# The S5 mixer of a two-layer trunk: u of tiles 4 to 7 prepared earlier, gelus of tiles 2 and 3 one by one, and another order of GEMM steps and u

## The chip, the cores and the metric

The kernel runs on one core of a Trainium2 chip. The metric is the device time of one execution in microseconds (us), as the median of several runs. TensorE (PE) multiplies, ScalarE (ACT) and VectorE (DVE) work element by element, GpSimd (POOL) does a little, and SyncE (SP) issues most of the DMAs. Each engine works through its own instructions in the order in which they were written, and waits at an instruction until the semaphores that it names are high enough.

## The reference

A trunk of two layers on a sequence of 256 positions and a width of 2048, each layer a token mixer and an MLP. Layer 0 has differential attention, layer 1 an S5 mixer (a grouped diagonal state space):

```python
h = rmsnorm(x, norm_mix[1])
u = h.reshape(B, S, 128, 16)                                  # 128 groups of 16 channels
bu_re, bu_im = einsum('sgc,gpc->sgp', u, bb_re), einsum('sgc,gpc->sgp', u, bb_im)
x_re, x_im = associative_scan(...)                            # x[s] = a * x[s-1] + bu[s], complex, 64 states a group
y = einsum('sgp,gcp->sgc', x_re, cr) - einsum('sgp,gcp->sgc', x_im, ci) + d_skip * h
val, gate = split(gelu(y) @ w_glu, 2)                         # 2048 x 4096
x = x + val * sigmoid(gate)
x = x + relu(rmsnorm(x) @ w1)**2 @ w2
```

## The kernel before

All GEMMs stream their weights from DRAM through one list of chunks (two k-tiles of 128 rows by 512 columns, 512 KB). A chunk lands in `raw`, ScalarE casts it to `wh`, VectorE subtracts to get the remainder `wl`, and TensorE multiplies in three passes (L201 to L203, or L265 and L269 in the MLP's first half). A chunk is prepared up to three ahead of its use. While a GEMM runs, `pump()` is called at each k-tile and steps generators in the list `side`: these lay other work (attention heads, norms, the S5 tables) between the GEMM's instructions. What stands where is thus set by the order in which the Python code runs, with the delays that the generators yield.

The S5 mixer works on 16 tiles of 128 channels. The 256 positions of a tile are 64 chunks of 4. For tile j:

- `s5_u(j)` makes u for tiles j and j+1: four transposes of the residual (L1029), or, when it is given `diag`, four f32 matmuls with a diagonal of the norm's factors (L1031), into one PSUM bank; then 16 ScalarE copies (L1036) that spread it to the tile `vsb`. In the MLP the norm's factors aren't known yet, and `s5_scale` multiplies them in later on VectorE (L107).
- `s5_e(j)` is 16 matmuls (L1056) into one PSUM bank, and then 12 VectorE instructions: multiplications by a table, two scans (L1066), and the state `bc`, which is X[j].
- `s5_y` is 24 matmuls a tile (L1089) from u and X into a bank of its own ring, and at the end of its group 16 gelus (L1096) and a cast (L1100) on ScalarE. `s5_rest` makes the remainder on VectorE.
- `s5_dk(j)` is one ScalarE copy (L1020) that the scan of tile j reads. `s5_fetch(j)` loads the tables of tile j.
- The norm ahead of the mixer (`norm2`) takes two squares with sums on ScalarE (L422) behind each output block of the MLP.
- `glu_tile(j)` is the GEMM step of tile j: 4 f32 matmuls of 128x512 (L1122) with the gelus of tile j as the stationary operand, for the first 512 columns of value and gate.

`s5_phase` puts these in order, in a loop over j. A step has e of tile j+1, the remainder of tile j-3, a GEMM step (none at j = 0, 1 and 4), y of tile j, the copy for tile j+4, the gelus if tile j ends its group, u if j is 2, 4, 6 or 8, and the fetch of tile j+4. The three GEMM steps that are left over follow the loop. In the first two steps `keep_warm` adds 8 matmuls whose result nobody reads, and 18 and 4 stand at the phase's start.

In this phase `bank()` and `s5_u` take PSUM banks 4 and 5 in turn (`rings["sd"]`), so of e and u each takes the bank that the one before the last had. Tiles 0 to 3 get their u in the first MLP's last quarter (`early_u`, spawned by `done0` when the first of the four output blocks is finished); tiles 4 to 7 get it at the phase's start with banks of the ring "acc"; tiles 8 to 15 in the loop.

Of the kernel before, what the change touches and what calls it, by code (L numbers as in the profile page):

```python
# [16 lines left out]
P = 128  # L17
# [19 lines left out]
NCH = S // L  # L37
# [5 lines left out]
LAG = 3  # L43
# [14 lines left out]
def tile_trunk(  # L58
# [7 lines left out]
    v = nc.vector  # L66
# [13 lines left out]
    def nm(s):  # L80
        uid[0] += 1
        return f"{s}_{uid[0]}"
# [5 lines left out]
    def ring(kind):  # L88
        r = rings[kind]
        turn[kind] = (turn[kind] + 1) % len(r)  # L90
        return psum.tile([P, 512], F32, tag=f"bank{r[turn[kind]]}", name=nm(kind), bufs=1)
# [6 lines left out]
    def bank():  # L98
        return ring("sd")

    def tmp(shape, tag, bufs=None, dt=F32):
        if bufs is None:
            return sb.tile(shape, dt, tag=tag, name=nm(tag))
        return sb.tile(shape, dt, tag=tag, name=nm(tag), bufs=bufs)

    def mult(o, a, b):
        v.tensor_tensor(out=o, in0=a, in1=b, op=ALU.mult)  # L107

    def add(o, a, b):
        v.tensor_tensor(out=o, in0=a, in1=b, op=ALU.add)  # L110

    def sub(o, a, b):
        v.tensor_tensor(out=o, in0=a, in1=b, op=ALU.subtract)  # L113

    def tsc(o, a, s1, op0, s2=None, op1=None):
        if op1 is None:
            v.tensor_scalar(out=o, in0=a, scalar1=s1, scalar2=None, op0=op0)
        else:
            v.tensor_scalar(out=o, in0=a, scalar1=s1, scalar2=s2, op0=op0, op1=op1)
# [8 lines left out]
    def spawn(gen, delay=0):  # L128
        side.append([clock[0] + delay, gen])
# [11 lines left out]
    def until(cond):  # L141
        while not cond():
            assert side
            pump()
# [79 lines left out]
    def new_accs():  # L224
        return [ring("acc") for _ in range(NT)]
# [94 lines left out]
    def keep_warm(n):  # L320

        if n == 0:
            return
        a = ring("acc")
        for _ in range(n):
            pe.matmul(a, x1[3].h[:, 0, 0:P], x1[3].h[:, 0:2], start=True, stop=True)
# [683 lines left out]
    def s5_rooms():  # L1010

        for _ in range(4):
            dks.append(tmp([P, Q, NCH], "s1k", bufs=4))
            xps.append(tmp([P, 2, Q, NCH], "bc", bufs=4))
            pool_e.memset(dks[-1][:, :, 0:1], 0.0)
            pool_e.memset(xps[-1][:, :, :, 0:1], 0.0)

    def s5_dk(j):
        if j < NJ:
            act.copy(dks[j % 4][:, :, 1:], rr[:, j * Q:(j + 1) * Q, None].broadcast_to([P, Q, NCH - 1]))  # L1020

    def s5_u(j, diag=None, kind="sd"):

        ps = ring(kind).rearrange("p (i s) -> p i s", s=S)
        for i in range(2):
            for t in range(NT):
                o, xs = ps[:, i, t * P:(t + 1) * P], xres[t][:, (j + i) * P:(j + i + 1) * P]
                if diag is None:
                    pe.transpose(o, xs, ident)  # L1029
                else:  # L1030
                    pe.matmul(o, xs, diag[:, t], start=True, stop=True)  # L1031
        u = tmp([P, 2, Q, NCH], "vsb", bufs=4)
        pv = ps.rearrange("p i (k s) -> p i s k", s=L)
        for s in range(L):
            for q in range(Q):
                act.copy(u[32 * s:32 * s + 32, :, q], pv[32 * q:32 * q + 32, :, L - 1 - s])  # L1036
            yield s
        if diag is None:
            U[j] = u
        else:  # L1040
            U[j], U[j + 1] = u[:, 0], u[:, 1]

    def s5_scale(j, factor):
        u = U[j]
        uv = u.rearrange("p i q k -> p (i q) k")
        mult(uv, uv, factor[:, None, :].broadcast_to([P, 2 * Q, NCH]))
        U[j], U[j + 1] = u[:, 0], u[:, 1]

    def s5_e(j):
        te, to, tt, ct = tab[j]  # L1050
        u, dk, xp = U[j], dks[j % 4], xps[j % 4]
        pe_ = bank().rearrange("p (i q k) -> p i q k", i=2, q=Q)
        for i in range(2):
            for q in range(Q):
                for h in (slice(0, GP), slice(GP, P)):
                    pe.matmul(pe_[h, i, q], te[:, i, q, h], u[:, q], start=True, stop=True)  # L1056
        sh = [P, 2, Q, NCH]
        tw = tmp([P, 2] + sh[1:], "c5")
        t1, t2 = tw[:, 0], tw[:, 1]
        mult(t1, pe_, ct[:, 0:1].broadcast_to(sh))  # L1060
        mult(t2, pe_, ct[:, 1:2].broadcast_to(sh))
        add(t1[:, 0], t1[:, 0], t2[:, 1])
        sub(t1[:, 1], t1[:, 1], t2[:, 0])
        zz = tmp(sh, "s2k", bufs=7)
        for i in range(2):
            v.tensor_tensor_scan(out=zz[:, i].rearrange("p q k -> p (q k)"), data0=dk.rearrange("p q k -> p (q k)"),  # L1066
                                 data1=t1[:, i].rearrange("p q k -> p (q k)"), initial=0.0,
                                 op0=ALU.mult, op1=ALU.add)
        n = NCH - 1
        shn = [P, 2, Q, n]  # L1070
        w1, w2 = tmp(sh, "s2k", bufs=7), tmp(sh, "s2k", bufs=7)
        mult(w1[:, :, :, 0:n], zz[:, :, :, 0:n], ct[:, 0:1, :, 0:n].broadcast_to(shn))
        mult(w2[:, :, :, 0:n], zz[:, :, :, 0:n], ct[:, 1:2, :, 0:n].broadcast_to(shn))
        sub(xp[:, 0, :, 1:], w1[:, 0, :, 0:n], w2[:, 1, :, 0:n])
        add(xp[:, 1, :, 1:], w1[:, 1, :, 0:n], w2[:, 0, :, 0:n])
        X[j] = xp
# [30 lines left out]
    def s5_rest(j):  # L1107

        while rest and rest[0][0] <= j:
            _, blk, kk, n, g = rest.pop(0)  # L1110
            sub(blk.l[:, kk:kk + n], g[:, 0:n], blk.h[:, kk:kk + n].bitcast(F32))
            blk.ready = kk + n == KB
# [16 lines left out]
    def s5_phase(norm):  # L1129
        until(lambda: norm.done)  # L1130
        act.activation(warm_act, warm_act, AF.Gelu_apprx_tanh)
        keep_warm(WARM[0])
        sel = wp.tile([P, 2, NT, P], F32, tag="wl", name="sel", bufs=LIVE)
        ar, diag = sel[:, 0], sel[:, 1]
        for t in reversed(range(NT)):
            tsc(ar[:, t], sela.rearrange("p s r -> p (s r)"), norm.rstd[:, t:t + 1], ALU.mult)
        for t in range(NT):
            act.activation(diag[:, t], ident, AF.Copy, scale=norm.rstd[:, t:t + 1])
        prs = bank()[:, 0:NCH]
        for t in range(NT):  # L1140
            pe.matmul(prs, ar[:, t], selb[:, t], start=(t == 0), stop=(t == NT - 1))
        keep_warm(WARM[1])
        s5_scale(0, prs)
        s5_scale(2, prs)
        s5_e(0)
        for j in (4, 6):
            for _ in s5_u(j, diag, "acc"):
                pass
        groups = [(0,), (1,), (2, 3), (4, 5), (6, 7), (8, 9), (10, 11), (12, 13), (14,), (15,)]
        ys = {}  # L1150
        for grp in groups:
            gen = s5_y(grp)
            for j in grp:
                ys[j] = (gen, j == grp[-1])
        glu = 0
        for j in range(NJ):
            if j + 1 < NJ:
                s5_e(j + 1)
            s5_rest(j - 3)
            if j < 2:  # L1160
                keep_warm(WARM[2])
            if j in (2, 3) or j >= 2 + LAG:
                if glu == 0:
                    A["v"], A["g"] = new_accs(), new_accs()
                glu_tile(glu)
                glu += 1
            gen, end = ys[j]
            next(gen)
            s5_dk(j + 4)
            if end:  # L1170
                for _ in gen:
                    pass
            if j in (2, 4, 6, 8):
                for _ in s5_u(j + 6, diag):
                    pass
            s5_fetch(j + 4)
            pump()
        while glu < NJ:
            prep(GLU0 + 16 + glu - NJ + LAG)
            glu_tile(glu)  # L1180
            glu += 1
        s5_rest(NJ)
# [92 lines left out]

    def done0(u, ts):
        norm2.block(u, ts)
        if u == 0:
            spawn(early_u(), 4)
            spawn(early_tables(), 2)  # L1280
        if u == NB - 1:
            norm2.finish(slice(ts[0], ts[0] + 1))

    def early_u():
        for j in (0, 2):
            for _ in s5_u(j):
                yield 2
        s5_rooms()
        yield 2
        for j in range(4):  # L1290
            s5_dk(j)
            yield 2
# [28 lines left out]
    def evict_gate(accs, vs, u):  # L1321
# [6 lines left out]
        spawn(xT_block(x3[u], u, 2, norm3, "a"), 6)  # L1328

    s5_phase(norm2)  # L1330
    evict_gate(A["g"], first_vals, 0)
    for u in range(1, NB):
# [62 lines left out]
```

## Time and profile before

| | us |
|---|---|
| median of 3 runs | 2104.28 (2104.16 to 2104.45) |
| the profiled execution | 2101.04 |
| its span, from the first instruction to the last | 2099.3 |
| TensorE busy in the span | 2076.1 (99%) |
| VectorE busy | 1369.1 (65%) |
| ScalarE busy | 1061.4 (51%) |
| GpSimd busy | 122.9 (6%) |

The profiled execution lies 3.2 us below the median. A busy share is an average over the whole span: the S5 phase, some 120 us of it, has another mix than the GEMMs around it. The profile's granted clock of TensorE is 0.999 in the mean.

### The profile page before, as it was taken

The page shows a single profiled execution, that of the slowest core. Times are in us where ns is not written, and L with a number is a line of the kernel's source. Part 1 is how long each engine was busy: PE and PEld are TensorE (multiplying, and loading weights), DVE is VectorE, ACT ScalarE, POOL GpSimd, SP SyncE. Part 2 cuts the span into 40 slices and gives each one's busy share as a digit, 9 for nine tenths or more (in the row PEclk, how much of TensorE's full clock was granted, in tenths as well). Part 3 has the DMA queues.
Part 4 walks back from the last instruction along what each step waited for, and adds up shares of the span by engine and source line. Part 5 has one row for each costly group of instructions (what it writes and reads, how often), then busy time and mean ns, then how long its engine had stood idle before and what let it go on. Part 6 is the DMA issues. An engine that isn't in the chain of part 4 may idle for free.

```text
span 2099.3 us, 31788 instructions
## 1 busy us (share of the span) xinstructions
PE 2076.1 (99%) x12126; PEld 1763.8 (84%) x12126; DVE 1369.1 (65%) x2292; ACT 1061.4 (51%) x1640; POOL 122.9 (6%) x210
## 2 busy tenths in 40 slices
PE   8999999999999999999999999999999999999998
PEld 8899998888888888888887668888888888888886
DVE  5785656688678767767866865565556645645655
ACT  5545545555445444454566875444434434434443
POOL 2000200021021002100110000000000000000000
PEclk9999999999999999999999999999999999999999
DMA  7457765677776777687678765665565556555653
GB/s 244 157 193 241 248 178 184 214 229 267 237 240 233 273 238 222 225 276 235 208 266 310 274 215 187 200 201 199 189 195 189 189 193 191 178 204 181 200 192 131
DMA packets 230813, 452.57 MB, mean 216 GB/s; under 512 B 20818, under 2 KB 29348, under 8 KB 230660
## 3 DMA queue, kind: packets, MB, share of 16 engines
q1 hardware_dynamic: 217824, 415.29, 59.8%
q0 software_dynamic: 11440, 32.86, 4.9%
q10 hardware_dynamic: 1396, 2.39, 0.3%
q8 instruction: 95, 1.56, 0.3%
q14 instruction: 58, 0.48, 0.1%
HBM read 420.85 MB, written 41.68 MB: 220 GB/s over the span
## 4 chain that ended last, share of the span: by engine, by line
PE 91%; ACT 3%; DVE 3%; DMA 1%; issue 1%; SPq 0%; DVEq 0%; ACTq 0%
PE acc L265 21%; PE acc L201 15%; PE acc L202 15%; PE acc L203 15%; PE acc L269 11%; PE acc L1122 3%; PE acc L248 2%; PE acc L250 2%; PE acc L249 2%; DVE wl L113 1%; ACT wh L191 1%; PE y L1089 1%; ACT s2k L1096 1%; DMA raw<-in_a_w_in_dram 1%; ACT vsb L1036 1%
## 5 line engine op out<-in xcount | busy, mean ns | idle before, releaser
L113 DVE TENSOR_TENSOR wl<-raw,wh 128x1024 fp32r<-128x1024 f32 (+1 forms) x690 | 833.2, 1217 | 574.4 <-ACT wh L191 570.0
L191 ACT CAST wh<-raw 128x1024 fp32r<-128x1024 f32 (+1 forms) x690 | 712.9, 1047 | 631.0 <-PE acc L203 341.4
L201 PE MATMUL acc<-wh,x 128*128 128x512 f32 x832 | 326.8, 393 | 0.0
L203 PE MATMUL acc<-wh,x 128*128 128x512 f32 x832 | 324.0, 389 | 0.0
L202 PE MATMUL acc<-wl,x 128*128 128x512 f32 x832 | 324.0, 389 | 0.0
L265 PE MATMUL acc<-x,wh 128*128 128x512 f32 x1024 | 273.9, 394 | 2.8 <-DVE s2k L110 2.8
L265 PE MATMUL acc<-a,wh 128*128 128x512 f32 x1024 | 272.8, 393 | 0.0
L201 PE MATMUL acc<-wh,a 128*128 128x512 f32 x640 | 251.5, 393 | 0.0
L202 PE MATMUL acc<-wl,a 128*128 128x512 f32 x640 | 249.4, 390 | 0.1
L203 PE MATMUL acc<-wh,a 128*128 128x512 f32 x640 | 249.3, 390 | 0.0
L265 PEld LDWEIGHTS acc<-x,wh 128*128 128x128 f32 x1024 | 177.3, 189 | 28.9 <-DVE s2k L110 3.2
L265 PEld LDWEIGHTS acc<-a,wh 128*128 128x128 f32 x1024 | 177.3, 189 | 25.3 <-ACT s2k L1324 0.4
L203 PEld LDWEIGHTS acc<-wh,x 128*128 128x128 f32 x832 | 156.2, 188 | 32.9
L201 PEld LDWEIGHTS acc<-wh,x 128*128 128x128 f32 x832 | 156.3, 188 | 32.0 <-ACT vsb L1317 0.3
L202 PEld LDWEIGHTS acc<-wl,x 128*128 128x128 f32 x832 | 156.3, 188 | 31.8 <-issue 0.2
L269 PEld LDWEIGHTS acc<-a,wl 128*128 128x128 f32 x1024 | 152.8, 190 | 18.7
L269 PEld LDWEIGHTS acc<-x,wl 128*128 128x128 f32 x1024 | 152.4, 190 | 18.8
L269 PE MATMUL acc<-x,wl 128*128 128x256 f32 x1024 | 158.0, 282 | 0.0
L269 PE MATMUL acc<-a,wl 128*128 128x256 f32 x1024 | 157.5, 281 | 0.0
L248 PE MATMUL acc<-x,wh 128*128 128x256 f32 x512 | 148.4, 290 | 1.2 <-ACT wh L191 1.2
L249 PE MATMUL acc<-x,wh 128*128 128x256 f32 x512 | 145.4, 284 | 0.1
L250 PE MATMUL acc<-x,wl 128*128 128x256 f32 x512 | 145.5, 284 | 0.0
(246 smaller groups left out, 2105.8 us busy)
## 6 DMA issues: line engine op xcount, KB each, us to landing
raw<-in_mlp_w_dram SPq DMA_DIRECT2D x512, 512.0 KB
raw<-in_a_w_in_dram SPq DMA_DIRECT2D x94, 512.0 KB
raw<-in_b_w_glu_dram SPq DMA_DIRECT2D x64, 512.0 KB
raw<-in_a_w_out_dram SPq DMA_DIRECT2D x32, 512.0 KB
scr<-t POOLq DMA_DIRECT2D x32, 512.0 KB, 5.6
teo<-scr SPq DMA_DIRECT2D x32, 512.0 KB
t<-scr SPq DMA_DIRECT2D x16, 512.0 KB
pwr<-pwn SPq DMA_DIRECT2D x16, 256.0 KB
```

Source lines behind the costliest of these rows:

```text
L113: v.tensor_tensor(out=o, in0=a, in1=b, op=ALU.subtract)
L191: act.copy(h[:, sl], r[:, sl])
L201: pe.matmul(accs[t], lhs.h[:, k, ts], wh, start=first, stop=False)
L202: pe.matmul(accs[t], lhs.h[:, k, ts], wl, start=False, stop=False)
L203: pe.matmul(accs[t], lhs.l[:, k, ts], wh, start=False, stop=last)
L248: pe.matmul(o, wh[:, kk, cs], lhs.h[:, k], start=f and c % 2 == 0, stop=False)
L249: pe.matmul(o, wh[:, kk, cs], lhs.l[:, k], start=False, stop=False)
L250: pe.matmul(o, wl[:, kk, cs], lhs.h[:, k], start=False, stop=e and c % 2 == 1)
L265: pe.matmul(a[c], wh, lhs.hl[:, k].rearrange("p i s -> p (i s)"), start=first, stop=False)
L269: pe.matmul(a[c][:, S:], wl, lhs.h[:, k], start=False, stop=last)
L1036: act.copy(u[32 * s:32 * s + 32, :, q], pv[32 * q:32 * q + 32, :, L - 1 - s])
L1122: pe.matmul(accs[t], g[:, t * P:(t + 1) * P], raws[i][:, kk], start=j == 0, stop=j == NJ - 1)
```

## The change

The whole diff:

```diff
@@ s5_phase
         s5_scale(0, prs)
         s5_scale(2, prs)
+        rsb = tmp([P, NCH], "rsb", bufs=1)
+        v.tensor_copy(rsb, prs)
         s5_e(0)
-        for j in (4, 6):
-            for _ in s5_u(j, diag, "acc"):
-                pass
-        groups = [(0,), (1,), (2, 3), (4, 5), (6, 7), (8, 9), (10, 11), (12, 13), (14,), (15,)]
+        groups = [(0,), (1,), (2,), (3,), (4, 5), (6, 7), (8, 9), (10, 11), (12, 13), (14,), (15,)]
...
             s5_rest(j - 3)
+            if j in (0, 2):
+                s5_scale(j + 4, rsb)
             if j < 2:
                 keep_warm(WARM[2])
-            if j in (2, 3) or j >= 2 + LAG:
+            if 2 <= j < 6 or j >= 4 + LAG:
                 if glu == 0:
                     A["v"], A["g"] = new_accs(), new_accs()
                 glu_tile(glu)
...
-            if j in (2, 4, 6, 8):
-                for _ in s5_u(j + 6, diag):
+            if j in (3, 5, 7, 9):
+                for _ in s5_u(j + 5, diag):
                     pass
@@ the first MLP
     def done0(u, ts):
         norm2.block(u, ts)
+        if u < 2:
+            spawn(early_u(u), 4)
         if u == 0:
-            spawn(early_u(), 4)
             spawn(early_tables(), 2)
...
-    def early_u():
-        for j in (0, 2):
+    def early_u(u):
+        for j in (4 * u, 4 * u + 2):
             for _ in s5_u(j):
                 yield 2
+        if u == 0:
+            return
         s5_rooms()
         yield 2
         for j in range(4):
```

LAG is 3. The u of tiles 4 to 7 is made in the first MLP by transposes, behind its second output block, and scaled in the loop's steps 0 and 2 from a copy of the row factors in SBUF. Tiles 2 and 3 get their gelus one by one. GEMM steps stand in steps 2 to 5 and from 7 on, and u of tiles 8 to 15 in steps 3, 5, 7 and 9, at the end of a group, behind its gelus.

What this does to the order of the instructions is shown at three places. The first is ScalarE in the phase, around the copies of u for tiles 10 and 11 (vsb_12192 before, vsb_12308 after). Before:

```order
L1096 ACTIVATE s2k_12106<-y_11988 32x128 x16
L1100 CAST x_11848<-s2k_12106 128x2x256
L1020 COPY s1k_11344<-rr 128x4x63
L1036 COPY vsb_12192<-sd_12187 32x2x64 x16
L1020 COPY s1k_11348<-rr 128x4x63
L1096 ACTIVATE s2k_12274<-y_12161 32x128 x16
L1100 CAST x_12291<-s2k_12274 128x2x256
```

After:

```order
L1020 COPY s1k_11554<-rr 128x4x63
L1020 COPY s1k_11558<-rr 128x4x63
L1096 ACTIVATE s2k_12284<-y_12188 32x128 x16
L1100 CAST x_12301<-s2k_12284 128x2x256
L1036 COPY vsb_12308<-sd_12303 32x2x64 x16
L1020 COPY s1k_11562<-rr 128x4x63
L1020 COPY s1k_11566<-rr 128x4x63
```

Before, the copies stood ahead of the gelus of tiles 4 and 5 (s2k_12274); after, they stand behind them (s2k_12284).

The second is TensorE, from the u of tiles 10 and 11 on. Before, from its last matmul (sd_12187) on; the next e that takes its bank is e of tile 7, which follows when y of tile 5, eight rows long, is over:

```order
L1031 MATMUL sd_12187<-sel,xres_77 128x128
L1056 MATMUL sd_12214<-vsb_11748,teo_12036 64x64 x16
L1122 MATMUL acc_11980<-raw_11534,s2k_12106 128x512
L1122 MATMUL acc_11981<-raw_11534,s2k_12106 128x512
L1122 MATMUL acc_11982<-raw_11552,s2k_12106 128x512
L1122 MATMUL acc_11983<-raw_11552,s2k_12106 128x512
L1089 MATMUL y_12161<-vsb_11726,t_2145_11945 64x64 x2
```

After, from its last matmul (sd_12303) to e of tile 8 (sd_12393), which takes its bank:

```order
L1031 MATMUL sd_12303<-sel,xres_77 128x128
L1056 MATMUL sd_12330<-vsb_11451,teo_12147 64x64 x16
L1089 MATMUL y_12362<-vsb_11451,t_2159_12037 64x64 x2
L1089 MATMUL y_12362<-bc_11563,teo_12036 64x64 x4
L1089 MATMUL y_12362<-vsb_11451,t_2159_12037 64x64 x2
L1089 MATMUL y_12362<-bc_11563,teo_12036 64x64 x4
L1089 MATMUL y_12362<-vsb_11451,t_2159_12037 64x64 x2
L1089 MATMUL y_12362<-bc_11563,teo_12036 64x64 x4
L1089 MATMUL y_12362<-vsb_11451,t_2159_12037 64x64 x2
L1089 MATMUL y_12362<-bc_11563,teo_12036 64x64 x4
L1056 MATMUL sd_12393<-vsb_12130,teo_12214 64x64 x16
```

Between u and the e that takes its bank there was an e, a GEMM step and a y; now there is an e and a y, and the GEMM step stands behind.

The third is ScalarE in the first MLP's last quarter, behind the second output block. Before:

```order
L191 CAST wh_11322<-raw_11183 128x1024
L191 CAST wh_11360<-raw_11208 128x1024
L984 ACTIVATE t_2047_11343<-s2k_11315,gm 128x8x64 x2
L1020 COPY s1k_11344<-rr 128x4x63
L191 CAST wh_11382<-raw_11242 128x1024
L1020 COPY s1k_11348<-rr 128x4x63
L191 CAST wh_11406<-raw_11268 128x1024
```

After:

```order
L191 CAST wh_11322<-raw_11183 128x1024
L1036 COPY vsb_11349<-sd_11344 32x2x64 x4
L191 CAST wh_11354<-raw_11208 128x1024
L984 ACTIVATE t_2047_11343<-s2k_11315,gm 128x8x64 x2
L1036 COPY vsb_11349<-sd_11344 32x2x64 x4
L191 CAST wh_11379<-raw_11242 128x1024
L1036 COPY vsb_11349<-sd_11344 32x2x64 x4
L191 CAST wh_11406<-raw_11268 128x1024
```

Groups of four copies for tiles 4 and 5 (vsb_11349) now stand between the casts of the weight chunks, and the single copies of `s5_dk` have moved further behind.

## Rows read from the trace of the kernel before

**Rows 1.** The page, chain that ended last: shares of the span by engine.

```profile
PE 91%; ACT 3%; DVE 3%; DMA 1%; issue 1%; SPq 0%; DVEq 0%; ACTq 0%
```

**Rows 2.** Windows: stretch, length, busy us (instructions) of PE, PEld, DVE, ACT, POOL, then clock.

```profile
1129.73:1249.24 119.51, 114.68 (x1499) 75.55 (x1498) 93.88 (x181) 96.73 (x290) 0.00 (x0) 1.00 0.68 238
```

**Rows 3.** TensorE's waits, 1125 to 1260: who for whom, us, times, longest.

```profile
PE acc L1122 <- ACT s2k L1096: 4.5, 3, 2.1
```

**Rows 4.** VectorE timeline: start, us, line, operation, count, [idle before].

```profile
1136.48 1.29 DVE L107 TENSOR_TENSOR c<-sd,t 128x512 f32<-128x512 f32 x2 [0.79 <-PE sd L1056]
...
1141.76 1.28 DVE L107 TENSOR_TENSOR c<-sd,t 128x512 f32<-128x512 f32 x2
```

**Rows 5.** TensorE timeline, same columns: u, e, GEMM step, y, next e.

```profile
1195.49 1.16 PE L1031 MATMUL sd<-sel,xres 128*128 128x128 f32 x8
1196.58 1.15 PE L1056 MATMUL sd<-vsb,teo 128*64 128x64 f32 x32
1197.66 3.70 PE L1122 MATMUL acc<-raw,s2k 128*128 128x512 f32 x8
1201.29 0.34 PE L1089 MATMUL y<-vsb,t 128*64 128x64 f32 x4
...
1202.74 1.10 PE L1056 MATMUL sd<-vsb,teo 128*64 128x64 f32 x32
```

**Rows 6.** ScalarE timeline: single gelus, pair's gelus, cast, s5_dk, copies of u10.

```profile
1146.57 4.64 ACT L1096 ACTIVATE s2k<-y 32x64 f32<-32x64 f32 x16
...
1163.91 6.55 ACT L1096 ACTIVATE s2k<-y 32x128 f32<-32x128 f32 x16 [1.57 <-PE y L1089]
...
1170.50 0.62 ACT L1100 CAST x<-s2k 128x512 fp32r<-128x512 f32 x1
1171.02 0.40 ACT L1020 COPY s1k<-rr 128x252 f32<-128x252 f32 x1
1171.44 4.28 ACT L1036 COPY vsb<-sd 32x128 f32<-32x128 f32 x16
```

**Rows 7.** TensorE timeline: e3, two GEMM steps with waits, e7, e12.

```profile
1148.38 1.10 PE L1056 MATMUL sd<-vsb,teo 128*64 128x64 f32 x32
...
1151.27 3.70 PE L1122 MATMUL acc<-raw,s2k 128*128 128x512 f32 x8 [1.78 <-ACT s2k L1096]
...
1170.52 3.70 PE L1122 MATMUL acc<-raw,s2k 128*128 128x512 f32 x8 [2.15 <-ACT s2k L1096]
...
1175.77 1.15 PE L1056 MATMUL sd<-vsb,teo 128*64 128x64 f32 x32
...
1208.86 1.10 PE L1056 MATMUL sd<-vsb,teo 128*64 128x64 f32 x32
```

**Rows 8.** TensorE timeline: four transposes of u in the first MLP.

```profile
1068.53 0.60 PE L1029 MATMUL sd<-ident,xres 128*128 128x128 f32 x4
1068.88 0.48 PE L201 MATMUL acc<-wh,a 128*128 128x512 f32 x1
1069.20 0.40 PE L202 MATMUL acc<-wl,a 128*128 128x512 f32 x1
1069.43 0.40 PE L203 MATMUL acc<-wh,a 128*128 128x512 f32 x1
```

**Rows 9.** Windows, columns as in rows 2: in the MLP.

```profile
1094.26:1108.46 14.20, 14.09 (x63) 11.59 (x63) 11.29 (x14) 9.39 (x14) 0.53 (x1) 1.00 0.77 262
```

**Rows 10.** All waits, 1050 to 1130: those of TensorE.

```profile
PEld acc L202 <- DVE wl L113: 0.5, 1, 0.5
```

**Rows 11.** TensorE timeline: the kernel's first GEMM.

```profile
7.85 0.58 PE L248 MATMUL acc<-x,wh 128*128 128x256 f32 x1 [1.24 <-ACT wh L191]
...
9.17 0.41 PE L249 MATMUL acc<-x,wh 128*128 128x256 f32 x1
9.38 0.41 PE L250 MATMUL acc<-x,wl 128*128 128x256 f32 x1
...
11.93 0.28 PE L249 MATMUL acc<-x,wh 128*128 128x256 f32 x1
12.05 0.28 PE L250 MATMUL acc<-x,wl 128*128 128x256 f32 x1
```

## The prediction

> **What bounds the kernel now.** I read the chain of work that ended last first: 91% of the span is TensorE's [rows 1], so only what TensorE waits for, or is given to do, counts. The change lies in the S5 stage. It begins at 1129.73 us with the 18 keep-warm matmuls and is over when the next weight GEMM starts at 1249.24, 119.51 us later; TensorE is busy in 114.68 of these, ScalarE in 96.73, VectorE in 93.88 [rows 2]. TensorE bounds the stage, but the two others are so full that the order of their work decides whether it waits. What it waits for in the list of waits are three gelus of ScalarE, 4.5 us in all [rows 3]. Only these, and TensorE's own work, can be won.
>
> The stage has two regimes. At first VectorE sets the pace: a tile costs it 5.28 us, from 1136.48 to 1141.76 [rows 4], TensorE less. Later TensorE does: u takes 1.09 us, e 1.08, the GEMM step of a tile 3.63, y 1.45 [rows 5], so two tiles with a u cost about 13.4. On ScalarE the gelus take 4.64 us for a single tile and 6.55 for a pair, the cast behind a pair 0.52 to the next start, the 16 copies of a u 4.28 [rows 6]: 11.35 for two tiles. That fits, if nobody waits for the end of it.
>
> In fact somebody does. e of every tile and u take PSUM banks 4 and 5 in turn, so the second e behind a u writes the bank that u's copies read. The copies of the u of tiles 10 and 11 end at 1171.44 + 4.28 = 1175.72 [rows 6], and e of tile 7 starts at 1175.77 [rows 7]. Before, this wait is just met: ScalarE has u's copies *ahead* of the next pair of gelus.
>
> **The change part by part.** *u of tiles 4 to 7 into the MLP.* It takes two u's from TensorE and their copies, 8.56 us, from ScalarE out of the stage's start. The u's lay beside VectorE's first tile, so on TensorE nothing is won by that: y of tile 0 still waits for VectorE. But the gelus of tile 0 start as soon as y of tile 0 is done, and the first GEMM step then starts behind e of tile 3, at 1148.38 + 1.08 instead of at 1151.27: 1.8 us won [rows 7]. In the MLP the u's come back as 8 transposes: four take 0.35 us, and the matmul behind them 0.32 instead of 0.23 [rows 8], so 0.45, twice: **+0.9** on TensorE's path.
>
> ScalarE must fit 8.56 us of copies between the MLP's casts, 7.5 of it (seven groups of four) ahead of the squares of the third block, less four s5_dk copies (1.6) that move behind. Between 1094.26 and the squares at 1108.46 it is busy for 9.39 of 14.20 us [rows 9]: 4.8 are idle and some 1.1 don't fit. Whether that reaches TensorE this trace doesn't show. The nearest row is its own: the eight groups for tiles 0 to 3, put between casts of the same quarter in the same way, came with one wait of TensorE for a weight there, 0.5 us [rows 10]. Bounds: -0.5 (the transposes fill that wait) and +1.1. I take 0, between -0.5 and the same 0.5 again.
>
> *Copy of the row factors, scalings in the loop.* The copy falls into the 0.79 us for which VectorE waits ahead of its first e [rows 4]. A scaling is one multiplication of 128x512, 0.64 us by two of that shape [rows 4]; it stands in VectorE's queue behind e of tile 1, and again behind that of tile 3, and y of tile 2 and of tile 4 wait for what is behind it. It is in the walk.
>
> *Order of u, gelus and e.* Now the walk, in us from the stage's start, with these durations and 0.05 to 0.1 from an end to who waits. VectorE ends tile 1 at 17.3, tile 2 at 23.2, tile 3 at 28.5, tile 4 at 34.4, tile 5 at 40.0. TensorE: e3 from 18.65 (1148.38 [rows 7]), GEMM 0 to 23.3, y2 to 24.9, e4, GEMM 1, y3 to 31.1, u8 to 32.2, e5, GEMM 2, y4 to 38.5. ScalarE: gelus of tile 3 from 31.2 to 35.8, cast, copies of u8 to 40.45. Now e6 must have the bank of u8: it waits from 38.5 to 40.5, **2.0 us**; then GEMM 3, and y5 to 46.7.
>
> Then u10, e7, no GEMM step at j = 6 (its condition leaves it out), y6: TensorE is done at 50.4. ScalarE has the pair's gelus first, from 46.75 to 53.3, the cast, and only then u10's copies, to 58.1. e8 waits for the bank from 50.4 to 58.15: **7.75 us**. GEMM 4, whose gelus are long done, is queued behind e8 on TensorE and can't help.
>
> From there the pattern repeats. y7 ends at 64.4; ScalarE needs 6.55 + 0.52 + 4.28 = 11.35 to the end of u12's copies, TensorE only u12, e9, GEMM 5 and y8, 7.3, till it stands at e10: **4.1 us**, and once more at e12 for u14, **4.1 us**. e12 starts at 93.5. Before, it starts at 1208.86 [rows 7], which is 79.1. From here on no u is left, and both kernels run the same sequence at TensorE's pace. **Stage: +14.4.** That is the four new waits (17.95) less the two long gelu waits that vanish, and some tenths at the start.
>
> *TensorE's clock.* The kernel's first GEMM shows the two levels: its 128x256 matmuls start 0.21 us apart at 9.17 and 0.12 apart at 11.93, some 4 us into that GEMM, whose first waited at 7.85 [rows 11]. These spacings are 1.2 and 2.4 GHz (the granted clock on the page reads full in that slice too). A wait of 2.15 us in the stage didn't cost it: the GEMM step behind it takes 3.70, as the others [rows 5, 7]. Waits of 4.1 and 7.75 this trace does not hold. A fall costs about those 4 us at half speed, 1.9 lost, and behind e8 it reaches the end in full, since y7 starts the next gelus. Bounds: no fall, 0; one behind each of three waits, 5.7. I take one, behind the wait that lies furthest from the 2.15 that did nothing: **+1.9**.
>
> The Trainium skill (TensorE: Matmul & The Clock Gate, "What's actually happening") makes the low clock the default, which activity lifts and idleness brings back. The start of this trace agrees (0.21, then 0.12 us). By its rule, if each of the three long waits counts as idle, the sum would have 5.7 here in place of 1.9.
>
> Sum: 14.4 + 0.9 + 0 + 1.9 = **+17.2 us**. The profiled execution's own 2101.04 us would become 2118.2; it lies 3.2 below the median of the runs, 2104.28, and the shift is the same for both: **2121.5**.
>
> **The rivals.** (a) *The waits, but no fall of the clock*: 15.3, so 2119.6. For it: the 2.15 us that did nothing. Against it: 7.75 is more than three times that. (b) *Two or three falls*: 4.1 is twice 2.15, and the waits recur every 17.6 us; +19.1 or +21.0, with the 1.1 of late casts up to 22.1, so 2123.4 to 2126.4. (c) *No wait for the bank*: if e found its bank free, the 17.95 would be gone: 14.4 - 17.95 + 0.9 = -2.7, so 2101.6, not slower. It decides at one point: the change pays as long as the four waits together stay under 2.7 us. For it: ScalarE is idle for 22.8 us of the stage [rows 2]. Against it: the built order has u10's copies behind the gelus, and e8 behind only e7 and y6; and e7 of the kernel before starts 0.05 us after the copies of its bank end. (d) *Only the start changes*, because the steps at j = 3, 5, 7, 9 and the missing GEMM step at 6 only shift work that TensorE has to do anyway: -1.8 + 0.9, so 2103.4. For it: TensorE's work in the stage is otherwise the same. It needs u's copies to be done in time as in (c).
>
> **How the numbers follow.** One fall: 0.40. (a) 0.27. (b) 0.25. (c) and (d) together 0.08, of which 0.02 for a gain of more than 0.2% (4.2 us, about what a measurement of this kernel can tell from no change; (c) would have to win 1.5 more) and 0.06 for within it. Slower by over 0.2%: 0.92. The range: lower end from (a), with -0.5 in the MLP and 1.5 off the walk's waits, 2117.6; upper end from (b), all three falls and the late casts, 2126.4.
>
> **What the profile would show.** Right: TensorE idle four times ahead of e, about 2, 7.8, 4.1 and 4.1 us, each ended by the copies of a u on ScalarE; the stage at 134 to 140 us; of the waits for gelus only the last, half a us, left; behind the longest wait a GEMM step of over 4 us, and in the MLP transposes at two more places with no long wait of TensorE. Wrong: if e8 starts behind y6 while ScalarE still copies u10, the bank isn't what holds it, and (c) is right. If the stage is longer by 14 and the whole by much more, the MLP's casts are late, and my 0 there failed. If all GEMM steps take 3.6 us, the clock did not fall.

## The result, and the profile after

The changed kernel takes 2125.64 us in the median of 4 runs (2125.32 to 2126.7), the kernel before 2104.22 in the median of 4: it is slower by 21.4 us. The ratio over these runs is 1.011, with a 95% interval of 1.0099 to 1.0122; on 2104.22 that is 23.1 us, 20.8 to 25.7. The forecast was 17.2 us, 2121.5, with 2117.6 to 2126.4 as its range. The direction and the place are right, the size is 4.2 to 5.9 us short: the median of the changed kernel lies just inside the range, but 23.1 us on the 2104.28 that the forecast started from are 2127.4, above it. Medians and ratios, here and below, leave out two runs of the kernel before in a slow state, at 3466 and 4206 us, beside experiments 5 to 8.

I read the waits of TensorE in the stage first (1125 to 1280; columns as in [rows 3]):

```profile
PE sd L1056 <- ACT vsb L1036: 18.6, 4, 8.0
PE y L1089 <- issue: 1.9, 1, 1.9
PE acc L1122 <- ACT s2k L1096: 0.5, 1, 0.5
```

The two long gelu waits of [rows 3] are gone. In their place stand four waits of e (L1056) for copies of u (L1036), 18.6 us. The second line is y of tile 0 (the releaser is given only as "issue"; what it waits for is shown below).

Next, the window of the whole stage, from the 18 keep-warm matmuls to the next weight GEMM, with the columns of [rows 2]:

```profile
1132.84:1275.16 142.32, 121.28 (x1484) 79.34 (x1482) 95.32 (x185) 91.24 (x275) 0.00 (x0) 0.90 0.57 201
```

It was 119.51 long and is 142.32: +22.8. TensorE's busy time rose by 6.6 us, although it has two u's less to do here, and its granted clock fell from 1.00 to 0.90. So there are two losses: time in which TensorE waits, and time in which it works at a lower clock.

TensorE's timeline shows both. These are e6, e8, e10 and e12, each with what follows it, and the y behind the slow GEMM steps:

```profile
1174.15 1.15 PE L1056 MATMUL sd<-vsb,teo 128*64 128x64 f32 x32 [2.13 <-ACT vsb L1036]
1175.23 3.70 PE L1122 MATMUL acc<-raw,s2k 128*128 128x512 f32 x8
...
1192.02 1.98 PE L1056 MATMUL sd<-vsb,teo 128*64 128x64 f32 x32 [7.98 <-ACT vsb L1036]
1193.93 5.00 PE L1122 MATMUL acc<-raw,s2k 128*128 128x512 f32 x8
1198.86 0.34 PE L1089 MATMUL y<-vsb,t 128*64 128x64 f32 x4
...
1212.04 1.98 PE L1056 MATMUL sd<-vsb,teo 128*64 128x64 f32 x32 [4.22 <-ACT vsb L1036]
1213.95 5.22 PE L1122 MATMUL acc<-raw,s2k 128*128 128x512 f32 x8
...
1219.11 0.34 PE L1089 MATMUL y<-vsb,t 128*64 128x64 f32 x4
...
1232.31 1.98 PE L1056 MATMUL sd<-vsb,teo 128*64 128x64 f32 x32 [4.24 <-ACT vsb L1036]
1234.22 5.33 PE L1122 MATMUL acc<-raw,s2k 128*128 128x512 f32 x8
...
1239.48 0.34 PE L1089 MATMUL y<-vsb,t 128*64 128x64 f32 x4
```

In brackets stand the waits: 2.13, 7.98, 4.22 and 4.24, where the walk had 2.0, 7.75, 4.1 and 4.1. Behind the first, e and the GEMM step run as before (to the next start 1.08 and 3.63). Behind the three long ones e takes 1.91 to the next start, the GEMM step 4.93, 5.16 and 5.26: 0.83 + 1.30, 0.83 + 1.53 and 0.83 + 1.63 more, that is 2.1, 2.4 and 2.5 us, 7.0 in all.

That the clock is at fault shows in the windows of the step behind 2.13, of the wait of e8, and of the slow steps behind the three long waits (PEclk is the seventh quantity, behind POOL):

```profile
1175.23:1178.86 3.63, 3.63 (x13) 1.44 (x9) 3.45 (x7) 0.00 (x0) 0.00 (x0) 1.00 0.85 321
1184.04:1192.02 7.98, 0.01 (x2) 0.00 (x0) 4.29 (x9) 7.64 (x26) 0.00 (x0) 0.64 0.89 343
1192.02:1198.86 6.84, 6.84 (x40) 3.73 (x41) 4.71 (x9) 0.68 (x2) 0.00 (x0) 0.67 0.01 6
...
1212.04:1219.11 7.07, 7.07 (x41) 3.88 (x41) 4.94 (x10) 0.68 (x2) 0.00 (x0) 0.64 0.30 119
1232.31:1239.48 7.17, 7.17 (x40) 3.88 (x41) 5.04 (x10) 0.67 (x2) 0.00 (x0) 0.64 0.36 144
```

The granted clock goes down while TensorE waits for e8's bank (mean 0.64), and is 0.64 to 0.67 in the three stretches behind the long waits: a mean of a part at 1.2 GHz and a part at 2.4. The lower level itself stands in two shorter windows, the end of the wait and e8:

```profile
1188.00:1192.00 4.00, 0.00 (x0) 0.00 (x0) 0.40 (x2) 3.81 (x16) 0.00 (x0) 0.50 0.80 322
1192.02:1193.93 1.91, 1.91 (x32) 1.79 (x32) 0.00 (x0) 0.68 (x2) 0.00 (x0) 0.50 0.05 21
```

Why e8 waits is seen on ScalarE's timeline:

```profile
1180.52 6.50 ACT L1096 ACTIVATE s2k<-y 32x128 f32<-32x128 f32 x16 [5.71 <-PE y L1089]
1187.06 0.62 ACT L1100 CAST x<-s2k 128x512 fp32r<-128x512 f32 x1
1187.70 4.27 ACT L1036 COPY vsb<-sd 32x128 f32<-32x128 f32 x16
```

It had been idle for 5.71 us; then come the pair's gelus, the cast, and only behind these the copies of u10, which end at 1191.97. e8 starts at 1192.02. The order is as forecast, and so are the durations of [rows 6] but one: the copies start 0.64 us behind the start of the cast, where the walk took 0.52.

The rest of the loss lies outside. The two profiled executions differ by 25.6 us in span (25.7 in device time): 22.8 in the stage, 1.5 from the first transpose of u in the MLP to the stage, 1.65 ahead of that transpose, where both kernels run the same instructions, and -0.3 behind the stage. The 1.65 is a fall of the clock too. It lies behind a wait at a GEMM of the MLP's first half (L265), well ahead of the transposes. Here are the wait in the trace of after, then the same matmuls in before (first line) and in after:

```profile
817.06 0.73 PE L265 MATMUL acc<-x,wh 128*128 128x512 f32 x2 [2.24 <-DVE s2k L110]
```

```profile
817.18:820.51 3.33, 3.33 (x16) 2.84 (x17) 2.58 (x6) 1.16 (x3) 2.21 (x4) 1.00 1.05 397
817.06:821.98 4.92, 4.92 (x17) 4.07 (x17) 3.48 (x7) 2.28 (x5) 2.03 (x4) 0.65 0.97 362
```

They take 4.92 us at a granted clock of 0.65, before 3.33 at 1.00 behind a wait of 1.71. The change has no part in it: of the ten traces of this document three have the clock down at this place (after, experiments 4 and 7), seven don't, the changed kernel's own second trace (experiment 8) among these.

The two executions also lie 3.2 us below and 1.1 above the medians of their kernels: 25.7 - 3.2 - 1.1 = 21.4. That goes with the granted clock as well. In 38 runs of the kernel before, beside the experiments, the 7 with a mean granted clock of 0.999 take 2100.5 us in the mean, the 20 with 0.998 2103.3, the 11 with 0.997 2105.1; the profiled one has 0.999. Where the others lose their clock no trace shows.

One loss in the stage was foreseen by none of my cases. At the start TensorE's y of tile 0 waits 1.94 us, since the u's of tiles 4 to 7 no longer fill that time, and the e behind it is slow. The first row is VectorE's, which writes what that y reads and ends at 1144.62; then come TensorE's:

```profile
1144.20 0.42 DVE L113 TENSOR_TENSOR bc<-s2k,s2k 128x252 f32<-128x252 f32 x1
```

```profile
1144.72 0.62 PE L1089 MATMUL y<-bc,teo 128*64 128x64 f32 x8 [1.94 <-issue]
...
1146.91 1.93 PE L1056 MATMUL sd<-vsb,teo 128*64 128x64 f32 x32
```

From this y to the end of e it takes 4.05 us, in experiment 8, where the clock stays up, 2.53. Part of that is made up at the next y, whose wait of 0.36 in experiment 8 is gone here: e3 starts 19.43 us into the stage, where the walk, [rows 7] and experiment 8 have 18.65, 0.8 more. So the stage is 14.4 (walk) + 0.6 (longer waits) + 7.0 + 0.8 = 22.8.

### The profile page after: what moved, and what is told of

It reads as the page before. It is cut to its first block, busy times and chain, and to the rows that moved or that the text cites. A ratio compares the mean times of both kernels' runs of the same rounds, so it can differ in the third digit from the quotient of the medians.

```text
span 2124.9 us, 31793 instructions
## 1 busy us (share of the span) xinstructions
PE 2084.9 (98%) x12118; PEld 1769.0 (83%) x12118; DVE 1371.2 (65%) x2296; ACT 1064.2 (50%) x1657; POOL 123.0 (6%) x210
## 3 DMA queue, kind: packets, MB, share of 16 engines
q8 instruction: 95, 1.56, 0.3%
## 4 chain that ended last, share of the span: by engine, by line
PE 92%; ACT 4%; DVE 2%; issue 1%; DMA 1%; DVEq 0%; SPq 0%; ACTq 0%
PE acc L265 21%; PE acc L201 15%; PE acc L202 15%; PE acc L203 15%; PE acc L269 11%; PE acc L248 3%; PE acc L250 3%; PE acc L249 3%; PE acc L1122 2%; ACT vsb L1036 1%; ACT s2k L1096 1%; DVE wl L113 1%; PE y L1089 1%; ACT wh L191 1%; PE sd L1056 1%
## 5 line engine op out<-in xcount | busy, mean ns | idle before, releaser
L265 PE MATMUL acc<-x,wh 128*128 128x512 f32 x1024 | 275.2, 396 | 3.3 <-DVE s2k L110 3.3
L265 PE MATMUL acc<-a,wh 128*128 128x512 f32 x1024 | 272.7, 393 | 0.0
L265 PEld LDWEIGHTS acc<-x,wh 128*128 128x128 f32 x1024 | 178.2, 190 | 29.8 <-DVE s2k L110 3.7
L265 PEld LDWEIGHTS acc<-a,wh 128*128 128x128 f32 x1024 | 177.3, 189 | 25.0
```

Source lines behind the costliest of these rows:

```text
L265: pe.matmul(a[c], wh, lhs.hl[:, k].rearrange("p i s -> p (i s)"), start=first, stop=False)
```

## The experiments

The theory: in an odd step the pair's gelus stand ahead of u's copies on ScalarE, the second e behind that u needs the bank that these copies read, and a long wait there also lowers TensorE's clock. The rivals: the copies in the MLP are late; the missing GEMM step at 6 leaves TensorE without work; ScalarE's load, not the bank, is the limit; the slow steps have nothing to do with the waits. The changed kernel is "after" in what follows. The first four experiments ran on one chip (median of 19 runs of the kernel before: 2102.92), the other four on another (19 runs: 2103.39); ratios are to the kernel before beside them.

**1. u at the even steps again.**

```diff
-            if j in (3, 5, 7, 9):
-                for _ in s5_u(j + 5, diag):
+            if j in (2, 4, 6, 8):
+                for _ in s5_u(j + 6, diag):
```

> The changed kernel, with u of tiles 8 to 15 at the even steps again (steps 2, 4, 6 and 8, six tiles ahead). Everything else of the change stays. Theory (e waits for the bank that u's copies read, because these are queued behind the pair's gelus): with the copies ahead of a pair's gelus the waits of 8.0, 4.2 and 4.2 us are gone, and with them the three falls of the clock behind them (7.05 us). Left is one wait of some 2.4 us at e of tile 5, where u of tile 8 stands behind a single gelu, and one of 2.1 us for gelus. The stage should be within 2 us of that of the kernel before, and the time 2104.2 + 0.7 (walk) + 0.9 (transposes in the MLP) + 0.8 (slow y and e at the start) = about 2106.6 us, 2104 to 2109. Rival A (the copies of u in the first MLP are late and cost most): about 2120 us, with the stage short and the MLP long. Rival B (the GEMM steps two tiles behind, with none at step 6, leave TensorE without work): the waits stay at step 6 and the time is above 2113 us.

Measured: 2104.67 us, ratio 1.0006 (0.9997 to 1.0015). The stage is 121.58 long. Its waits of over 2 us:

```profile
1165.99 1.57 PE L1056 MATMUL sd<-vsb,teo 128*64 128x64 f32 x32 [2.14 <-ACT vsb L1036]
1167.49 4.90 PE L1122 MATMUL acc<-raw,s2k 128*128 128x512 f32 x8
...
1187.92 3.70 PE L1122 MATMUL acc<-raw,s2k 128*128 128x512 f32 x8 [2.13 <-ACT s2k L1096]
```

Nearly the whole loss is gone with this one part undone, although the MLP's copies, the single gelus and the missing GEMM step are all still there. Rivals A and B fall. Two waits of nearly the same length here have different effects: behind 2.14 the clock fell (1.57 and 4.90), behind 2.13 it didn't (3.70).

**2. The same order, u in another bank.**

```diff
-                for _ in s5_u(j + 5, diag):
+                for _ in s5_u(j + 5, diag, "y"):
```

> The changed kernel with one word more: u of tiles 8 to 15 takes its PSUM bank from the two of y (6 and 7) instead of from the two of e (4 and 5). Order and work of every engine are the same. Theory (the bank that u's copies read holds e): e never waits for copies; instead u takes turns with y, and y waits for the gelus of the pair before: by the same walk 4.7 us once, then twice 1.1. The stage becomes 12.5 us shorter than in the changed kernel, and of the falls of the clock one is left (behind the 4.7): 2125.6 - 12.5 - 4.9 = about 2108 us, 2105 to 2112. Rival (the order on ScalarE alone is what costs, whichever bank is used, or ScalarE's load is too high for the stage): within 3 us of 2125.6.

Measured: 2108.71 us, ratio 1.0025 (1.0014 to 1.0036); the stage 124.70, which is 17.6 shorter than after. TensorE's waits:

```profile
PE y L1089 <- ACT s2k L1096: 6.0, 3, 4.4
PE y L1089 <- issue: 1.9, 1, 1.9
PE acc L1122 <- ACT s2k L1096: 0.5, 1, 0.5
```

No e waits any more. ScalarE does the same work in the same order as in after, so its order and its load by themselves cost at most the 5 to 6 us by which this kernel is still behind that of before; some 17 us of the loss hang on the bank that e and u share. The new waits of y for gelus are 4.40, 0.81 and 0.80 (4.7, 1.1 and 1.1 were expected), and of these only behind the 4.40 is the clock down (e 1.92).

**3. u ahead of the gelus in the odd steps.**

```diff
-            if end:
-                for _ in gen:
-                    pass
             if j in (3, 5, 7, 9):
                 for _ in s5_u(j + 5, diag):
                     pass
+            if end:
+                for _ in gen:
+                    pass
```

> The changed kernel, still with u at the odd steps, but u and its copies are issued ahead of the gelus of the same step instead of behind them. Theory (in an odd step both the gelus and the copies become ready together and TensorE soon needs both; whichever stands second on ScalarE is waited for): the waits at e vanish but for one of 1.9 us, and the GEMM steps wait for gelus instead, by the walk 1.9, 5.5, 3.8 and 3.8 us. The stage is only some 2.4 us shorter than in the changed kernel: about 2123 us, 2120 to 2126. Rival (only the place behind the gelus is at fault): the waits are gone and the time is 2101 to 2106 us.

Measured: 2122.95 us, ratio 1.0098 (1.0085 to 1.0112).

```profile
PE acc L1122 <- ACT s2k L1096: 15.1, 5, 5.3
PE y L1089 <- issue: 2.3, 2, 1.9
PE sd L1056 <- ACT vsb L1036: 1.9, 1, 1.9
```

The waits moved from e to the GEMM steps. So it isn't the place behind the gelus as such: whichever of the two ScalarE does second in an odd step is late, since both become ready together and TensorE soon needs both. With u at the even steps (experiment 1) the copies are done ahead of the next gelus.

**4. TensorE kept at work in the waits.** y's matmuls are issued again, into the same place and with the same values.

```diff
-            for q in range(Q):
+            for q in [q for _ in range(1 + fill.get(j, 0)) for q in range(Q)]:
...
-            gen = s5_y(grp)
+            gen = s5_y(grp, {6: 5, 8: 2, 10: 2})
```

> The changed kernel, with y's matmuls issued again with the same operands into the same place (same values) while TensorE would wait: 5 times more for tile 6 (7.0 us), twice more for tiles 8 and 10 (2.8 us each). They end before the copies for which e waits, so no wait moves; TensorE is just not idle in it, 0.8, 1.4 and 1.4 us left of the 8.0, 4.2 and 4.2. Theory (the idle time in front of e lowers TensorE's clock, and each fall costs 2.1 to 2.5 us in the e and the GEMM step behind): e takes 1.15 in place of 1.98 us there and the GEMM steps 3.7 in place of 5.0 to 5.3, and the time falls by about 7 us to 2118.6, 2117 to 2120. Rival A (the slow GEMM steps come from something else than the waits, such as contention for SBUF): 2125.6. Rival B (the work added delays e): above 2125.6.

Measured: 2120.09 us, ratio 1.0084 (1.007 to 1.0098); after has 1.011 (from 1.0099), so 5 to 6 us less, but by two sets of runs, with intervals that all but touch. The trace is clearer. e6 with its GEMM step, then e10 and e12:

```profile
1174.72 1.15 PE L1056 MATMUL sd<-vsb,teo 128*64 128x64 f32 x32 [2.15 <-ACT vsb L1036]
1175.81 5.40 PE L1122 MATMUL acc<-raw,s2k 128*128 128x512 f32 x8
...
1212.81 1.15 PE L1056 MATMUL sd<-vsb,teo 128*64 128x64 f32 x32 [1.45 <-ACT vsb L1036]
1213.89 3.70 PE L1122 MATMUL acc<-raw,s2k 128*128 128x512 f32 x8
...
1230.71 1.15 PE L1056 MATMUL sd<-vsb,teo 128*64 128x64 f32 x32 [1.42 <-ACT vsb L1036]
1231.79 3.70 PE L1122 MATMUL acc<-raw,s2k 128*128 128x512 f32 x8
```

Where the waits were filled, e takes 1.15 and the GEMM step 3.70 (behind e8 as well: 1.10 and 3.70), and the granted clock over these stretches is 1.00. So the slow steps come from TensorE's own idleness, and rival A of this experiment falls. The stage is 4.4 us shorter, not 7.0: here the unfilled 2.15 ahead of e6 cost 1.7 (5.40 in place of 3.70), and the filling ran 0.6 us past the end of u10's copies, since TensorE stood still within it for 1.56 us ("issue").

**5. The other part alone: u of tiles 4 to 7 in the MLP, the rest as before.**

```diff
-        for j in (4, 6):
-            for _ in s5_u(j, diag, "acc"):
-                pass
+        rsb = tmp([P, NCH], "rsb", bufs=1)
+        v.tensor_copy(rsb, prs)
...
+            if j in (0, 2):
+                s5_scale(j + 4, rsb)
...
-    def early_u():
-        for j in (0, 2):
+    def early_u(u):
+        for j in (4 * u, 4 * u + 2):
...
```

> The kernel before with one part of the change alone: u of tiles 4 to 7 in the first MLP, with the copy of the row factors and the two scalings in the loop. Groups of gelus, steps of u and of the GEMM stay as before. Theory (this part moves almost nothing; the loss is made by the odd steps): in the MLP 8 transposes, +0.9 us, and no late casts; in the stage the first GEMM step starts 1.8 us sooner and keeps 1.7 of it; if TensorE's clock falls behind the 1.9 us for which y of tile 0 waits, 0.8 comes back. So 0 to -0.8: within 1 us of the kernel before on the same chip. Rival (the copies in the MLP delay casts, and that is part of the 21 us): 3 us or more slower, with waits of TensorE for weights or casts in the MLP.

Measured: 2101.2 us, ratio 0.9991 (0.9982 to 1.0). The stage is 117.65, 1.9 shorter than before, and in the MLP TensorE's weight loads wait 1.2 us for a weight's remainder, before 0.5 [rows 10]. The loss isn't here; if anything this part wins a little.

**6. The same, with 16 keep-warm matmuls in step 0 in place of 8.**

```diff
-                keep_warm(WARM[2])
+                keep_warm(WARM[2] * (2 - j))
```

> As the run before it (u of tiles 4 to 7 in the first MLP alone), with 16 keep-warm matmuls in place of 8 in step 0, which fill the 1.9 us for which TensorE waits ahead of y of tile 0. Theory (that wait sometimes lowers the clock): e of tile 2 never takes over 1.2 us, and the time is 0 to 0.8 us below that of the run before it, a candidate that is as fast as the kernel before or 1 us faster. Rival (the slow e there has another cause, the clock not being lowered by this wait): e of tile 2 takes 1.6 to 1.9 us as in the changed kernel.

Measured: 2101.36 us, ratio 0.9991 (0.9982 to 1.0). y of tile 0 is no longer in the list of waits (the one of 0.4 us left there is y of tile 1's, and experiment 5 has it too), and e of tile 2 takes 1.10. But in the profile of experiment 5 it took 1.10 too, behind the full 1.94, so this pair shows no gain: it bounds the start's fall to less than these runs can tell. Neither version is clearly faster than the kernel before (0.1%, with 1.0 at the interval's end); they are the fastest of the study.

**7. The odd steps alone, on the kernel before.**

```diff
-            if j in (2, 4, 6, 8):
-                for _ in s5_u(j + 6, diag):
+            if j in (3, 5, 7, 9):
+                for _ in s5_u(j + 5, diag):
```

> The kernel before with the other part alone: u at steps 3, 5, 7 and 9, five tiles ahead, in place of 2, 4, 6 and 8, six ahead. u of tiles 4 to 7, the gelus' groups and the GEMM steps stay. Theory (u behind the gelus of an odd step makes e wait for its bank): with the pair of tiles 2 and 3 also at an odd step there are four such waits, by the walk 8.1, 4.5, 4.5 and 4.5 us, and one of 1.7 for a gelu: the stage is 19.3 us longer than before, and four falls of the clock cost 2.2 to 2.5 each, 9.5: 28.8 us slower, a ratio of 1.0137 (1.011 to 1.015), more than the whole change. Rival (it takes the missing GEMM step at 6 or the MLP's copies too): a ratio below 1.006.

Measured: 2130.34 us, ratio 1.0135 (1.0121 to 1.0149). The waits of e are 8.00, 4.26, 4.26 and 4.24:

```profile
PE sd L1056 <- ACT vsb L1036: 20.8, 4, 8.0
PE acc L1122 <- ACT s2k L1096: 2.4, 2, 1.8
```

This part alone does more harm than the whole change. The rest of the change gives 4 to 5 us back, probably by the single gelus for tiles 2 and 3: with a pair the first wait, at e6 of this kernel, is 8.0, with single gelus 2.1. No run has the single gelus alone.

**8. The changed kernel again.**

> The changed kernel again, on the chip of these runs. Theory (a wait of about 2 us lowers TensorE's clock in some executions and not in others, one of about 4 us or more in each): the four waits at e are the same to 0.1 us, and the three long ones again have e at 1.9 to 2.0 and a GEMM step of 4.9 to 5.4 us behind; behind the waits of 1.9 (y of tile 0) and 2.1 (e of tile 6) the durations may differ from the first profile. Time 1.010 to 1.012 of the kernel before. Rival (the falls don't hang on the wait's length): some long wait has no slow step behind it.

Measured: 2126.27 us, ratio 1.0114 (1.0101 to 1.0128). This is the same loss of 23 us (22.9 by the medians, 24.0 by the ratio). The waits of e are 2.15, 8.00, 4.25 and 4.23, as in the first trace to 0.03; the clock is not the same:

```profile
1142.80 0.62 PE L1089 MATMUL y<-bc,teo 128*64 128x64 f32 x8 [1.94 <-issue]
...
1144.30 1.10 PE L1056 MATMUL sd<-vsb,teo 128*64 128x64 f32 x32
...
1171.47 1.15 PE L1056 MATMUL sd<-vsb,teo 128*64 128x64 f32 x32 [2.15 <-ACT vsb L1036]
1172.55 5.40 PE L1122 MATMUL acc<-raw,s2k 128*128 128x512 f32 x8
```

At y of tile 0 the same wait of 1.94 did nothing this time (e 1.10, in the first trace 1.93), and at e6 a wait of 2.15 cost 1.7 (5.40, in the first trace 3.70). Behind the three long waits the clock is down again, at 2.6 us each.

All traces side by side. "MLP" is from the first transpose of u to the stage, "behind" from the stage's end to the span's end; in us. The third column has TensorE's weight loads (PEld) in the MLP stretch that wait for VectorE's remainder of a weight, as in [rows 10]: the sum, and how many.

| kernel | MLP | weight waits | stage | behind |
|---|---|---|---|---|
| before | 61.20 | 0.5, 1 | 119.51 | 850.1 |
| after | 62.66 | 1.1, 2 | 142.32 | 849.7 |
| 1 even steps | 63.49 | 1.6, 3 | 121.58 | 849.8 |
| 2 other bank | 62.15 | 0.5, 1 | 124.70 | 849.8 |
| 3 u ahead of gelus | 62.64 | 1.1, 2 | 139.50 | 849.7 |
| 4 filled waits | 62.92 | 1.2, 2 | 137.89 | 849.6 |
| 5 MLP part alone | 62.77 | 1.2, 2 | 117.65 | 849.7 |
| 6 and more warm | 62.51 | 1.0, 2 | 118.01 | 849.5 |
| 7 odd steps alone | 61.05 | 0.4, 1 | 146.91 | 850.0 |
| 8 after again | 62.13 | 0.5, 1 | 144.20 | 849.8 |

The eight kernels with u of tiles 4 to 7 in the MLP have 62.66 there in the mean, the two without 61.1: that part costs 1.5 us.

## Where the prediction was right, and which of its terms failed

The mechanism was right; the step that failed is the clock's term of the sum. It stood at one fall and +1.9 us, and the trace has 7.0 behind three waits and 0.8 at the start in its place. The stage came out at 142.32 us, longer than the 134 to 140 that were named as the sign of being right.

*The waits.* Right in place, cause and size: 2.0, 7.75, 4.1 and 4.1 were forecast, 2.13, 7.98, 4.22 and 4.24 measured. Of the 0.6 between them 0.36 is the 0.12 between the cast's start and that of the copies, three times: the 0.52 was read ahead of a smaller copy [rows 6], and u's copies start 0.64 behind (1187.06 and 1187.70). That the bank is the cause is shown by experiment 2, that the odd steps bring it about by 1 and 7. Rivals (c) and (d) are out: e8 doesn't start behind y6 while ScalarE still copies u10.

*The clock.* This is the term that was mis-sized. Rival (b) with three falls is what happened, and one more fall at the start. I put it at one fall and +1.9, because the 2.15 us of [rows 7] had cost nothing and I placed the bound between 4.1 and 7.75. It was 7.0 behind the three long waits and 0.8 behind y of tile 0. Two things failed. First, one harmless wait of 2.15 was taken as a sign for 4.1, and it wasn't even a sign for 2.15: of the six waits of 2.13 to 2.15 in these ten traces three cost 1.6 to 1.7 us and three nothing, while all 14 waits of 3.70 or more cost something. Second, the price of a fall. I took 4 us at half speed from [rows 11], so 1.9; it was 2.1 to 2.5 in the trace of after. Three falls at the measured price are 5.1 over my term. That the range still reached up to the measured median is owed to its upper end, which held three falls and late casts, and not to the one fall that I forecast. [Rows 11] also show the two levels by their spacings alone: the granted clock reads 1.00 in that stretch (9.17 to 9.60), whereas in the stage it reads 0.50 where the matmuls are slow.

The Trainium skill (TensorE: Matmul & The Clock Gate, "What's actually happening") has the low clock as the default to which idleness leads back. The trace of after agrees for the wait of e8, in which the granted clock goes from 1.00 (1184.04 to 1186.00) to 0.50 (1188.00 to 1192.00). The same section of the Trainium skill says that the monitor doesn't keep step with the kernel, so that the point of a change varies between runs. Experiment 8 agrees, with the same wait of 1.94 ahead of y of tile 0 and no slow e behind it, where the first trace has one.

*The start.* The walk had y of tile 0 waiting for VectorE, rightly, and said that nothing is won there; it didn't ask what stops when the u's no longer fill that wait. The cover that went was TensorE's clock: 0.8 in the first trace, nothing in the second.

*The MLP.* 0.9 for the transposes and 0 for late casts were forecast; 1.5 in the mean were measured, within the bounds given. The transposes are right and the 0 is half a us too low: where the MLP has one weight wait, as before, the part costs 0.9 to 1.1 (experiments 2 and 8), and where it has two, 1.3 to 1.9 (after and experiments 3 to 6). The second one in after is

```profile
1119.29 0.19 PEld L202 LDWEIGHTS acc<-wl,a 128*128 128x128 f32 x1 [0.63 <-DVE wl L113]
```

and VectorE had waited 3.33 us for the cast of that weight, which stands on ScalarE behind copies of u and the squares of the third block.

*The sum.* 17.2 forecast. Add 0.6 for the waits, 7.0 - 1.9 and 0.8 for the clock and 0.6 for the MLP, and it is 24.3; the two profiled executions differ by 25.7, of which 1.65 lie ahead of any changed instruction, so 24.0. The ratios, 23.1 and in experiment 8 24.0 us, fit that; the 21.4 between the medians of four runs each is at the low end. That the forecast was made as a shift from one execution is right only as far as that execution is typical. With its granted clock of 0.999 the one of before was among the fastest, and one trace can't show that.

## What to carry to other kernels

When two pieces of work of one engine become ready in the same step, and another engine soon needs both, their order chooses which wait remains: here 18.6 us at one place or 17.0 at others. Put them into different steps. Before the copies that empty a PSUM bank are moved, ask who writes that bank next and what is queued ahead of the copies: another bank was worth some 17 us here. Price a wait of TensorE with what it does to the clock too: each wait of 4.2 us or more in the changed kernel cost 2.1 to 2.6 us on top. A single harmless wait says little about the next one of its length.

## What the runs showed of the hardware

A wait of TensorE of 3.70 to 8.00 us in the stage was followed by slow matmuls 14 times out of 14, at a cost of 1.5 to 2.9 us. Of the six waits of 2.13 to 2.15 us three were; the seven kernels' traces that have the 1.94 ahead of y of tile 0 show it three times (after and experiments 2 and 4) and four times not. Waits of 0.8 and 1.4 to 1.9 us elsewhere in the stage (experiments 2, 3, 4 and 7, and [rows 7]) had no such effect, but at the GEMM of the MLP's first half (L265) one of 1.77 did in experiment 4, as did those of 2.24 and 2.64 in after and experiment 7; 0.96 to 2.04 there in the other seven traces did not. The length of a wait of some 2 us doesn't decide it. Nor does the cost grow with the wait: 7.98 cost 2.1, 4.24 cost 2.5 in the same trace.

The fall can also come late. In experiment 8 e6 itself still takes 1.15 us behind its wait, and only the GEMM step behind it is slow. The granted clock of that GEMM step is 0.67:

```profile
1172.55:1177.80 5.25, 5.25 (x12) 2.03 (x8) 5.03 (x10) 0.00 (x0) 0.00 (x0) 0.67 0.59 202
```
